# Weight layouts from the host, a first product paced by its loads, and program order on TensorE, ScalarE and VectorE in a one-core hybrid decoder layer

## The chip, the core and the metric

The kernel runs on one core of a Trainium2 chip. Its time is the device time of one execution on that core, in microseconds (us); what the host does with arrays before the launch is not in it. The core's engines run beside each other, each through its own list of instructions in order: TensorE (PE) for matmuls, VectorE (DVE), ScalarE (ACT) and GpSimd (POOL) for elementwise work, SyncE (SP) for issuing most of the DMAs. An instruction waits on semaphores for what it reads and for the buffers it writes.

## What is computed

One decoder layer on x of 256 positions by 2048 channels, all in float32:

```
x = x + 1/2 * SwiGLU_1(RMSNorm(x))             # FFN1, inner width 5632
h = RMSNorm(x); p = h @ W_in                   # columns: q|k, v, o, i, f gates, S5 input u
y = [ mLSTM heads | S5 groups ] @ W_out        # mixer
x = x + y
x = x + 1/2 * SwiGLU_2(RMSNorm(x))             # FFN2
out = RMSNorm_final(x)
swiglu(x) = (silu(x @ w1) * (x @ w3)) @ w2
```

The mLSTM part has four heads in chunks of 64 positions, after a causal convolution of width 4 and a silu on q and k. The S5 part is 64 groups of 16 channels, each driving a diagonal complex state of 64, with a scan over the positions, then a gelu and a gate through `w_glu`.

## The kernel before

**Products.** A float32 product is made from three passes of PE. Each weight tile, two blocks of 128 rows by 512 columns (512 KB, `wraw`), is split into a high part `whi` by an ACT cast (line 157) and a low part `wlo` by a DVE subtraction (line 159); the activations are kept as `xh` and `xl` in the same way. `step_tok` then issues twelve matmuls of 128x512 (line 177): four with whi and xh, four with whi and xl, four with wlo and xh. One such step, over two blocks of rows, is the unit in which the kernel counts. `gemm_ch` does the same for products with channels on partitions (lines 225, 226, 231), 24 matmuls of 128x256 a step.

**Loads ahead.** `weights` (line 143) keeps three further steps in flight (`AHEAD`): the DMA, cast and split of step i+3 are written into the program ahead of the matmuls of step i, with four buffers each of wraw, whi and wlo. The list of steps for that is `plan`. The last 512 columns of FFN2 are not in it; `tail` makes them in two halves of 256 columns, each of five tiles, by loads, casts (line 435), splits (line 436) and matmuls (lines 480 to 482) of its own, with an evacuation between the halves (line 445) and squares on ACT (line 323).

**Hooks.** After each step `tick` runs what `after(n, fn)` has put n steps ahead, and takes tasks from a background list at a rate: S5's tables during FFN1 (`s5_params`, `per_j`), S5's channel tasks in the mixer at `S5_RATE` tasks a step (`s5`: load, drive, scan, unrotate, emit, act, for eight groups j).

**Stages.** A setup; the first product of FFN1 (`start`), which takes x in its natural layout in four blocks, transposes them on PE (line 341, eight of 128x128 a block) between its steps, and takes squares of x on ACT; FFN1 until about 756 us; the mixer until about 1106 us, in the order U (S5's input, two halves, with the gate matmuls of line 928 between), O, QK, V, `w_out` for the heads' half, `w_glu`, `w_out` for S5's half; FFN2 until about 1801 us; the tail. In the mixer `gates` runs in three parts, `conv(hf, i)` for eight blocks, `scores(h)` for four heads (their masked products land in Dm, line 966), `heads(c)` and `heads_T(c)` for two pairs of heads (hml, line 1030, is the low part that `w_out` reads), `evac_glu` behind `w_glu`.

**Order.** SP's instructions stand in program order. On the other engines a scheduler orders the instructions by its own estimate of times, except in `start`, where PE, ACT and DVE are in program order too:

```
ET = mybir.EngineType
with tc.manual_schedule(engines={ET.SP}):
    _Layer(ctx, tc, a, out).run()
```

## Time and profile before

| what | us |
| --- | --- |
| median of 3 runs (1839.41 to 1839.99) | 1839.96 |
| the profiled execution, its own time | 1839.91 |
| its span | 1838.2 |
| PE busy | 1821.5 |
| DVE, ACT, POOL busy | 1064.4, 818.1, 348.9 |

The span is from the first to the last instruction; the 1.7 us beyond it lie around the profiled instructions. Busy time of PE counts pipelined matmuls by their modelled ends, so a PE that is busy without a break can still differ in the spacing of its matmuls; the granted clock (PEclk) says at how much of full speed it ran. A wait is put down to the semaphore that came last.

### The profile page before, as it was taken

What the parts mean: (1) busy time and instruction counts of PE and PEld (TensorE: products, weight loads), DVE (VectorE), ACT (ScalarE), POOL (GpSimd) and SP (SyncE); (2) the same over time, 40 slices, a digit from 0 to 9 for tenths busy, and PEclk for the clock granted to TensorE, in tenths of its full rate; (3) what the DMA queues carried; (4) which work ended last, traced back from release to release, by engine and by line L of the source; (5) the groups of instructions that cost most, each with busy time, mean ns of one, the idle gap of its engine ahead of it and who ended that gap; (6) DMA issues with size and microseconds to landing.
All of it is one profiled execution on the core that took longest, in us unless ns stands there. A gap on an engine that the chain in (4) does not pass through costs nothing.

```text
span 1838.2 us, 24018 instructions
## 1 busy us (share of the span) xinstructions
PE 1821.5 (99%) x9174; PEld 1527.0 (83%) x9174; DVE 1064.4 (58%) x1261; ACT 818.1 (45%) x982; POOL 348.9 (19%) x519
## 2 busy tenths in 40 slices
PE   9999999999999999999999999999999999999998
PEld 7888888888888888998977988888888888888887
DVE  5546855555555555578888665454544545454554
ACT  6444444334444445444454564444443334444343
POOL 4000799920000000065545100000000000000011
PEclk9999999999999999999999999999999999999999
DMA  8666676676666665767784556666665666666563
GB/s 275 196 186 185 192 217 214 213 242 196 196 197 195 188 198 195 198 181 208 184 211 149 190 189 201 193 192 189 189 187 192 193 194 191 189 193 186 193 193 128
DMA packets 185652, 358.26 MB, mean 195 GB/s; under 512 B 12064, under 2 KB 18336, under 8 KB 185408
## 3 DMA queue, kind: packets, MB, share of 16 engines
q1 hardware_dynamic: 181344, 344.51, 63.1%
q0 software_dynamic: 4048, 11.16, 1.7%
q8 instruction: 72, 1.18, 0.3%
q10 hardware_dynamic: 144, 1.05, 0.1%
q14 instruction: 44, 0.36, 0.1%
...
## 4 chain that ended last, share of the span: by engine, by line
PE 95%; DVE 2%; DMA 2%; issue 1%; ACT 0%; ACTq 0%; POOLq 0%; POOL 0%; SPq 0%; DVEq 0%
PE accb L177 84%; PE accb L225 2%; PE accb L231 2%; PE accb L226 2%; DVE wlo L159 1%; PE tpb L492 1%; DMA wraw<-in_w_in_dram 1%; PE tpb L341 0%; DMA wraw<-in_ffn_w_dram 0%; PE tpb L852 0%; PE accb L482 0%; PE accb L481 0%; PE accb L480 0%; PE tpb L891 0%; PE tpb L928 0%
## 5 line engine op out<-in xcount | busy, mean ns | idle before, releaser
L159 DVE TENSOR_TENSOR wlo<-wraw,whi 128x1024 fp32r<-128x1024 f32 x622 | 791.1, 1274 | 677.4 <-ACT whi L157 676.8
L157 ACT CAST whi<-wraw 128x1024 fp32r<-128x1024 f32 x622 | 654.4, 1053 | 885.3 <-PE accb L177 814.4
L177 PE MATMUL accb<-whi,xh 128*128 128x512 f32 x1536 | 603.5, 393 | 0.6 <-ACT whi L157 0.6
L177 PE MATMUL accb<-whi,xl 128*128 128x512 f32 x1536 | 598.9, 390 | 0.8 <-DVE xl L351 0.8
L177 PE MATMUL accb<-wlo,xh 128*128 128x512 f32 x1536 | 410.7, 389 | 0.0
L177 PEld LDWEIGHTS accb<-whi,xh 128*128 128x128 f32 x1536 | 289.0, 188 | 61.6 <-ACT whi L157 1.3
L177 PEld LDWEIGHTS accb<-whi,xl 128*128 128x128 f32 x1536 | 289.0, 188 | 60.3 <-DVE xl L351 1.6
L177 PEld LDWEIGHTS accb<-wlo,xh 128*128 128x128 f32 x1536 | 288.3, 188 | 60.1
L177 PE MATMUL accb<-whi,gh 128*128 128x512 f32 x664 | 259.8, 391 | 0.0
L177 PE MATMUL accb<-whi,gl 128*128 128x512 f32 x664 | 258.4, 389 | 0.0
L177 PE MATMUL accb<-wlo,gh 128*128 128x512 f32 x664 | 177.5, 389 | 0.0
L177 PEld LDWEIGHTS accb<-wlo,gh 128*128 128x128 f32 x664 | 124.6, 188 | 25.9
L177 PEld LDWEIGHTS accb<-whi,gh 128*128 128x128 f32 x664 | 124.6, 188 | 25.6
L177 PEld LDWEIGHTS accb<-whi,gl 128*128 128x128 f32 x664 | 124.7, 188 | 25.5
L1201 POOL TENSOR_TENSOR x<-x,fn 128x512 f32<-128x512 f32 x6 | 12.1, 2041 | 689.9 <-ACT junk L323 689.9
L703 POOL TENSOR_TENSOR tr<-s5rot,sp 128x128 f32<-128x128 f32 (+6 forms) x112 | 55.5, 496 | 160.2 <-DVE sp L643 156.7
L225 PE MATMUL accb<-xh,whi 128*128 128x256 f32 x256 | 63.5, 286 | 0.0
L226 PE MATMUL accb<-xl,whi 128*128 128x256 f32 x256 | 62.8, 283 | 0.0
L705 POOL TENSOR_TENSOR s5rot<-tr,tr 128x128 f32<-128x128 f32 (+6 forms) x112 | 61.0, 557 | 3.3
L704 POOL TENSOR_TENSOR tr<-s5rot,sp 128x128 f32<-128x128 f32 (+6 forms) x112 | 57.2, 511 | 0.0
L764 POOL DMA_DIRECT2D spillw<-s5w x16 | 8.6, 541 | 249.6 <-ACT s5w L735 239.2
L225 PEld LDWEIGHTS accb<-xh,whi 128*128 128x128 f32 x256 | 49.1, 192 | 0.8 <-issue 0.4
...
## 6 DMA issues: line engine op xcount, KB each, us to landing
wraw<-in_ffn_w_dram SPq DMA_DIRECT2D x528, 512.0 KB, 3.8
wraw<-in_w_in_dram SPq DMA_DIRECT2D x64, 512.0 KB, 5.7
wraw<-in_w_out_dram SPq DMA_DIRECT2D x32, 512.0 KB, 4.2
spillrot<-s5rot POOLq DMA_DIRECT2D x8, 512.0 KB, 5.4
...
s5rot<-spillrot SPq DMA_DIRECT2D x8, 512.0 KB, 6.9
...
wraw<-in_w_glu_dram SPq DMA_DIRECT2D x8, 512.0 KB, 3.7
```

The costliest lines, as they stand in the source:

```text
L157: nc.scalar.copy(hi, raw)
L159: nc.vector.tensor_sub(lo, raw, hi.bitcast(F32))
L177: nc.tensor.matmul(acc[t][:, :n], lhsT=x, rhs=wt, start=first and t not in seen, stop=last and t not in left)
L225: nc.tensor.matmul(o(nt), lhsT=wh[:, kk, ns(nt)], rhs=xh, start=st, stop=False, **kw)
L226: nc.tensor.matmul(o(nt), lhsT=wh[:, kk, ns(nt)], rhs=xl, start=False, stop=False, **kw)
L231: nc.tensor.matmul(o(nt), lhsT=wl[:, kk, ns(nt)], rhs=xh, start=False, stop=sp, **kw)
L492: nc.tensor.transpose(b[:, o:o + P], s[t][:, kt * P:(kt + 1) * P], self.ident)
L703: G.tensor_tensor(tr[0][:, :, :k], rv[:, 0, :, 0:k], u0, op=ALU.mult)
L704: G.tensor_tensor(tr[1][:, :, :k], rv[:, 1, :, 0:k], u1, op=ALU.mult)
L705: G.tensor_tensor(rv[:, a, :, k:2 * k], tr[0][:, :, :k], tr[1][:, :, :k], op=op)
L764: nc.gpsimd.dma_start(out=d, in_=t)
L1201: nc.gpsimd.tensor_tensor(self.x[c][:, t, :], self.x[c][:, t, :], self.fn[:, c * NC:(c + 1) * NC], op=ALU.mult)
```

## The change

**Layouts.** The host now hands over every weight as tiles of 512 KB in which each of the 128 partitions has 4 KB in a row, w_in's columns in the order in which the kernel uses them, x also as its transpose xT, all column vectors as one array of 128x112 (`cols`), the gate biases as one column, the gate weights with a partition's values in a row, S5's c tables already transposed and zero padded (1 MB where 0.5 MB were loaded), and the tail's weights as tiles (`w_last`). So the transposes of x in `start` (32, of which 24 stood behind the first product's first matmul), those of the vectors (lines 272, 294), and those of the c tables (line 734) are gone, and nine small DMAs of POOL became one.

**The first product.** `start` loads for each of its eight steps 256 KB of xT and the step's weights, splits both, and multiplies. xT has two buffers. The first weight tile comes in two halves. Warm-up matmuls are twelve at one place instead of eight and four. x in its natural layout is loaded during the next product, and squares, rstd and the first silu follow there.

**Order.** PE, ACT and DVE stand in program order throughout; POOL stays with the scheduler.

**Mixer tasks.** S5's low part (the subtraction to yl) is a task of its own, one round later, and the rate is 0.72 in place of 0.69. The gates come in five parts, a convolution block in three, scores of heads 0 and 1 within V's first half, heads(0), scores of 2 and 3, heads_T(0) in its second half, a scaling of the heads one step behind `heads`, `evac_glu` by pairs behind following steps.

The core of the diff:

```diff
-S5_RATE = 0.69
+S5_RATE = 0.72
...
-WARM = 8
-MORE_WARM = 4
+WARM = 12
...
+    def fetch(self, *step):
+        return self.split(self.load(*step))
+
+    def load(self, name, k, kk, c0, n, parts=1):
+        raw = self.wraw.tile([P, KK * NC], F32, name="wraw")[:, :kk * n].rearrange("p (k n) -> p k n", n=n)
+        m = kk // parts
+        for i in range(0, kk, m):
+            self.nc.sync.dma_start(out=raw[:, i:i + m, :], in_=self.wview(name, k, c0)[:, i:i + m, :])
+        return raw
+
+    def split_tiles(self):
+        return (self.whi.tile([P, KK * NC], F32R, name="whi"), self.wlo.tile([P, KK * NC], F32R, name="wlo"))
+
+    def split(self, raw, tiles=None, ks=None):
+        nc = self.nc
+        kk, n = raw.shape[1:]
+        hi, lo = (t[:, :kk * n].rearrange("p (k n) -> p k n", n=n) for t in tiles or self.split_tiles())
+        ks = ks or slice(0, kk)
+        nc.scalar.copy(hi[:, ks, :], raw[:, ks, :])
+        nc.vector.tensor_sub(lo[:, ks, :], raw[:, ks, :], hi[:, ks, :].bitcast(F32))
+        return hi, lo
...
+    def start(self, acc, fp):
+
+        nc = self.nc
         ET = mybir.EngineType
+        self.xh = [self.xTp.tile([P, 4, S], F32R, name=f"xh{c}") for c in range(4)]
+        self.xl = [self.xTp.tile([P, 4, S], F32R, name=f"xl{c}") for c in range(4)]
+        w, raw, ready = {}, {}, []
+
+        def load_xT(i):
+            raw[i] = fp.tile([P, NC], F32, name="s0").rearrange("p (k s) -> p k s", k=KK)
+            nc.sync.dma_start(out=raw[i], in_=self.a["xT"][:, KK * i:KK * (i + 1), :])
+
+        def load(i, parts=1):
+            w[i] = self.steps.pop(0)
+            w[i] = w[i], self.load(*w[i], parts=parts)
+
+        def split_x(k):
+            c, i = divmod(k, 4)
+            g, src = self.col("ffn1_norm", k), raw[k // KK][:, k % KK, :]
+            nc.scalar.activation(self.xh[c][:, i, :], src, AF.Copy, scale=g)
...
+        def prepare(i):
+            step, wr = w[i]
+            if i == 0:
+                tiles = self.split_tiles()
+                for kk in range(KK):
+                    split_x(kk)
+                    ready.append((step, self.split(wr, tiles, slice(kk, kk + 1))))
+                ready.pop()
+                return
+            if i < 8:
+                for kk in range(KK):
+                    split_x(i * KK + kk)
+            ready.append((step, self.split(wr)))
...
+            for i in range(2):
+                load_xT(i)
+                load(i, KK if i == 0 else 1)
+            prepare(0)
+            load_xT(2)
+            load(2)
+            prepare(1)
             for i in range(8):
-                M(i, W(i))
-                if i % 2 == 0 and i < 6:
-                    T(i // 2 + 1)
-                if i % 2 == 0 and i < 4:
-                    self.load_x(i // 2 + 2)
-                if i >= 4:
-                    self.sumsq(i - 4)
-        self.finish_rstd()
+                if i < 5:
+                    load_xT(i + 3)
+                if i + 3 < 10:
+                    load(i + 3)
+                if i < 7:
+                    prepare(i + 2)
+                else:
+                    prepare(9)
+                    self.load_x(0)
+                self.step_tok(acc, self.xs, [(i * KK, 0), (i * KK + 1, 0)], ready.pop(0)[1], NC, i == 0, i == 7)
+        self.ahead = ready
...
-    def wview(self, name):
-        return self.a[name][0].rearrange("(k p) n -> p k n", p=P)
+    def wview(self, name, k, c0):
+        c = WIN.index(c0) if name == "w_in" else c0 // NC
+        return self.a[name][c, k // KK]
...
-        vec0 = self.s5p.tile([KD, P], F32, name="vec0", tag="s5k0")
-        nc.sync.dma_start(out=vec0, in_=self.a["ffn1_norm"][0].rearrange("(k p) -> k p", p=P))
+        rows = sum(n for _, n in _COLS)
+        self.cols = c.tile([P, rows], F32, name="cols")
+        nc.sync.dma_start(out=self.cols, in_=self.a["cols"])
...
+                    s = []
+
+                    def silu(p1=p1, s=s):
+                        for t in range(TT):
+                            s.append(fp.tile([P, NC], F32, name=f"s{t}"))
+                            nc.scalar.activation(s[t], p1[t], AF.Silu, scale=self.rstd[:, t:t + 1])
                     if l == 1 and cc == 0:
-                        self.start(p1, w1, lambda k: self.cols0[:, k:k + 1])
+                        self.start(p1, fp)
+                        for i, n in ((1, 1), (2, 3), (3, 4)):
+                            self.after(n, lambda i=i: self.load_x(i))
+                        for i, n in enumerate((2, 3, 5, 6)):
+                            self.after(n, lambda i=i: self.sumsq(i))
+                        self.after(6, self.finish_rstd)
+                        self.after(6, silu)
                     else:
                         self.gemm_tok(p1, self.xs, w1, ks, cc * NC, NC)
-                    s = []
-                    for t in range(TT):
-                        s.append(fp.tile([P, NC], F32, name=f"s{t}"))
-                        nc.scalar.activation(s[t], p1[t], AF.Silu, scale=self.rstd[:, t:t + 1])
+                        silu()
...
-        craw = [sp.tile([P, NJ, 64], F32, name=f"craw{i}") for i in range(2)]
+        cT = sp.tile([P, 2, NJ, P], F32, name="cT")
...
-        load(out=self.wgr, in_=self.wview("w_in")[:, :, GATE0:GATE0 + 2 * H])
+        load(out=self.wgr, in_=self.a["wgr"])
...
-            load(out=craw[i], in_=self.a[nm][0].rearrange("(j r) h p -> (r h) j p", r=8))
+            load(out=cT[:, i], in_=self.a["cT"][i])
...
-                b2 = self.bank()
-                for ri in range(2):
-                    nc.tensor.transpose(b2[:, ri * P:(ri + 1) * P], stc[ri].rearrange("p g q -> p (g q)"), self.ident)
-                nc.scalar.copy(w2[:, 0:128], b2[:, 0:128])
-                nc.scalar.activation(w2[:, 128:256], b2[:, 128:256], AF.Copy, scale=-1.0)
+                nc.scalar.copy(w2[:, 0:128], cT[:, 0, j, :])
+                nc.scalar.activation(w2[:, 128:256], cT[:, 1, j, :], AF.Copy, scale=-1.0)
...
                 def act():
                     A.activation(yT[:, j, :], yT[:, j, :], AF.Gelu_apprx_tanh)
                     A.copy(yh[:, j, :], yT[:, j, :])
+
+                def low():
                     V.tensor_sub(yl[:, j, :], yT[:, j, :], yh[:, j, :].bitcast(F32))
-                return [load, drive, scan, unrotate, emit, act]
+                return [load, drive, scan, unrotate, emit, act, low]
...
-            for j in range(NJ + 1):
+            def both(f, g):
+                return lambda: (f(), g())
+            for j in range(NJ + 2):
                 now = s5_parts[j] if j < NJ else []
-                old = s5_parts[j - 1] if j else []
-                self.bg.extend(now[:3] + old[4:5] + now[3:4] + old[5:])
+                old = s5_parts[j - 1] if 0 < j <= NJ else []
+                low = s5_parts[j - 2][6] if j > 1 else None
+                if now:
+                    self.bg.append(both(low, now[0]) if low else now[0])
+                elif low:
+                    self.bg.append(low)
+                self.bg.extend(now[1:3] + old[4:5] + now[3:4] + old[5:6])
...
-            for i, part in zip((1, 8, 12), self.gates(ma, mp, gbank, rB, Dm, em)):
+            for i, part in zip((1, 2, 8, 11, 13), self.gates(ma, mp, gbank, rB, Dm, em)):
...
                 for i in range(4):
-                    self.after(1 + 2 * i, lambda hf=hf, i=i: conv(hf, i))
+                    for part in range(3):
+                        self.after(1 + 2 * i + part, lambda hf=hf, i=i, part=part: conv(hf, i, part))
...
+                self.after(1, lambda: scale_heads(c, den, ss))
+
+            def scale_heads(c, den, ss):
...
+                if c == 0:
+                    self.after(6, lambda: scores(0))
+                    self.after(7, lambda: scores(1))
...
                 if c == 0:
-                    for h, n in enumerate((1, 2, 5, 6)):
-                        self.after(n, lambda h=h: scores(h))
-                    self.after(4, lambda: heads(0))
-                    self.after(7, lambda: heads_T(0))
+                    self.after(3, lambda: heads(0))
+                    self.after(4, lambda: scores(2))
+                    self.after(5, lambda: scores(3))
+                    self.after(6, lambda: heads_T(0))
                 else:
                     self.after(1, lambda: heads(1))
                     self.after(4, lambda: heads_T(1))
...
+                if hf == 0:
+                    self.after(1, lambda: two(0))
+                    self.after(2, lambda: two(2))
+                else:
+                    two(0)
+                    self.after(1, lambda: two(2))
...
+        def scan_part():
             V.scalar_tensor_tensor(f, f, 0.0, e, op0=ALU.min, op1=ALU.subtract)
...
-            for h2 in range(2):
+        def matrix_part(h2):
+            if True:
...
-        return [rows_part, columns_part, matrix_part]
+        return [rows_part, scan_part, columns_part, lambda: matrix_part(0), lambda: matrix_part(1)]
...
-    with tc.manual_schedule(engines={ET.SP}):
+    with tc.manual_schedule(engines={ET.SP, ET.PE, ET.Activation, ET.DVE}):
...
+    a = {name: inputs[name] for name in _INS}
+    f = lambda name: _np.asarray(inputs[name][0])
+    cols = lambda v: v.reshape(-1, P).T
+    a["xT"] = f("x").T.reshape(KD, P, S).transpose(1, 0, 2)
...
+    win = [f("w_in")[:, c:c + NC] for c in WIN]
+    a["wgr"] = f("w_in")[:, GATE0:GATE0 + 2 * H].reshape(KD, P, 2 * H).transpose(1, 0, 2)
+    a["w_in"] = _np.concatenate(win, axis=1)[None]
+    W, k0 = NC // 2, HALVES[0] * 4
+    last = f("ffn2_w2")[k0 * P:, D - NC:].reshape(-1, 4, P, 2, W).transpose(3, 0, 2, 1, 4)
+    a["w_last"] = last
+    for name in _STEPS:
+        w = _np.asarray(a[name][0])
+        a[name] = w.reshape(w.shape[0] // (KK * P), KK, P, w.shape[1] // NC, NC).transpose(3, 0, 2, 1, 4)
+    return a
```

How instructions stand now, at three places; names are the program's, with the shape written (and how many times it stands in a row).

ACT near the end, before. `x_94` is the third block of x, whose evacuation and squares belong to the last full product; line 435 is the tail's cast.

```order
L323 ACTIVATE junk,ss<-x_93 128x512 x2
L157 CAST whi<-wraw 128x1024 x6
L435 CAST whi<-wraw 128x1024 x4
L435 CAST xh_14887<-wraw 128x1024
L323 ACTIVATE junk,ss<-x_94 128x512 x2
L435 CAST xh_14893<-wraw 128x1024
L435 CAST whi<-wraw 128x1024
L435 CAST xh_14899<-wraw 128x1024
```

ACT at the same place, after (line 468 is the tail's cast, 347 the square):

```order
L347 ACTIVATE junk,ss<-x_93 128x512 x2
L168 CAST whi<-wraw 128x1024 x7
L347 ACTIVATE junk,ss<-x_94 128x512 x2
L468 CAST whi<-wraw 128x1024 x5
L347 ACTIVATE junk,ss<-x_95 128x256 x2
L468 CAST xh_14793<-wraw 128x1024
L468 CAST xh_14799<-wraw 128x1024
L468 CAST xh_14805<-wraw 128x1024
L468 CAST xh_14811<-wraw 128x1024
L468 CAST whi<-wraw 128x1024
```

Four of the first half's five casts, and the first of the second half's, stood ahead of the squares of x_94; now all five stand behind them, and those of the second half behind the squares of x_95.

DVE between FFN1 and the mixer, before. Line 922 is the low part of the gate weights, line 410 an evacuation of FFN1; the evacuation of uT, line 809, comes 16 rows further down:

```order
L159 TENSOR_TENSOR wlo<-wraw,whi 128x1024
L922 TENSOR_TENSOR wg<-wgr,wg 128x16x4 x2
L159 TENSOR_TENSOR wlo<-wraw,whi 128x1024 x2
L410 SCALAR_TENSOR_TENSOR x_95<-accb,x_95 128x512 x2
L159 TENSOR_TENSOR wlo<-wraw,whi 128x1024
```

DVE after, in U's first half (line 829 is the evacuation of uT, line 951 the low part of the gate weights):

```order
L819 COPY rB<-tpb 128x256
L820 TENSOR_SCALAR hrstd<-rstd 128x2
L169 TENSOR_TENSOR wlo<-wraw,whi 128x1024
L829 TENSOR_TENSOR uT_6322<-accb,rB 128x2x128x2 x2
L951 TENSOR_TENSOR wg<-wgr,wg 128x16x4 x2
L169 TENSOR_TENSOR wlo<-wraw,whi 128x1024
```

The low part of the gate weights moved from FFN1's last steps to just behind the evacuation of uT, which waits for PE's last matmul ahead of the gate matmuls.

SP at the start, before (line 257 loads a block of x, 155 a weight tile):

```order
L256 DMA vec_96<-in_ffn_norm_dram 16x128
L257 DMA x_92<-in_x_dram 128x2x512
L155 DMA wraw<-in_ffn_w_dram 128x2x512 x2
L257 DMA x_93<-in_x_dram 128x2x512
L155 DMA wraw<-in_ffn_w_dram 128x2x512 x2
L257 DMA x_94<-in_x_dram 128x2x512
L155 DMA wraw<-in_ffn_w_dram 128x2x512 x2
L257 DMA x_95<-in_x_dram 128x2x512
L155 DMA wraw<-in_ffn_w_dram 128x2x512 x258
```

SP at the start, after (line 209 loads xT for one step, 157 a weight tile or half of one):

```order
L303 DMA cols<-in_cols_dram 128x112
L209 DMA s_226<-in_xT_dram 128x512
L157 DMA wraw<-in_ffn_w_dram 128x512 x2
L209 DMA s_231<-in_xT_dram 128x512
L157 DMA wraw<-in_ffn_w_dram 128x1024
L209 DMA s_245<-in_xT_dram 128x512
L157 DMA wraw<-in_ffn_w_dram 128x1024
L209 DMA s_257<-in_xT_dram 128x512
L157 DMA wraw<-in_ffn_w_dram 128x1024
```

A block of x of 512 KB for every two steps became 256 KB of xT for each step.

## Rows read from the trace of the kernel before

**Rows 1.** The page, part 1: busy us (share), instructions of each engine.

```profile
PE 1821.5 (99%) x9174; PEld 1527.0 (83%) x9174; DVE 1064.4 (58%) x1261; ACT 818.1 (45%) x982; POOL 348.9 (19%) x519
```

**Rows 2.** The chain of FFN2 from 1106 us: start, duration (us), work.

```profile
1106.11 43.54 PE accb L177 x192
```

**Rows 3.** Windows of 12 us, mixer: engines' busy us, PE clock, DMA share, GB/s.

```profile
820.00:832.00 12.00, 12.00 (x74) 9.17 (x73) 10.84 (x12) 1.48 (x2) 10.75 (x10) 0.86 0.54 144
...
940.00:952.00 12.00, 10.35 (x48) 8.28 (x46) 10.58 (x7) 5.22 (x8) 10.99 (x6) 1.00 0.72 206
952.00:964.00 12.00, 10.83 (x51) 8.47 (x52) 7.54 (x22) 4.85 (x12) 1.04 (x1) 0.86 0.76 218
964.00:976.00 12.00, 10.07 (x78) 8.10 (x76) 11.29 (x12) 4.59 (x8) 6.72 (x4) 1.00 0.27 89
976.00:988.00 12.00, 11.71 (x44) 9.43 (x45) 9.27 (x22) 7.59 (x17) 7.88 (x6) 0.86 0.67 225
```

**Rows 4.** Waits of PE from 820 to 1106: us in total, times, longest.

```profile
PE tpb L991 <- DVE Dm L966: 2.6, 1, 2.6
PE accb L177 <- DVE hml L1030: 2.2, 1, 2.2
```

**Rows 5.** Groups by line, ACT and DVE, 820 to 1106: busy, mean ns | idle before.

```profile
L157 ACT CAST whi<-wraw 128x1024 fp32r<-128x1024 f32 x87 | 90.4, 1046 | 67.8 <-PE accb L177 34.9 <-DMA wraw<-in_w_in_dram 20.9 <-PE accb L226 10.9
...
L159 DVE TENSOR_TENSOR wlo<-wraw,whi 128x1024 fp32r<-128x1024 f32 x89 | 129.1, 1460 | 43.0 <-ACT whi L157 43.0
```

**Rows 6.** The page, parts 5 and 6: DVE's splits; w_in loads, us to landing.

```profile
L159 DVE TENSOR_TENSOR wlo<-wraw,whi 128x1024 fp32r<-128x1024 f32 x622 | 791.1, 1274 | 677.4 <-ACT whi L157 676.8
...
wraw<-in_w_in_dram SPq DMA_DIRECT2D x64, 512.0 KB, 5.7
```

**Rows 7.** The chain of the start, 0 to 37 us: start, duration, work.

```profile
1.25 4.67 DMA x<-in_x_dram
...
11.65 8.45 DMA wraw<-in_ffn_w_dram
...
25.75 0.87 PE tpb L341 x8
```

**Rows 8.** Timeline of PE, first product: start, duration (us), work.

```profile
8.49 0.50 PE L177 MATMUL accb<-whi,xh 128*128 128x512 f32 x1 [0.57 <-ACT whi L157]
...
33.73 1.07 PE L177 MATMUL accb<-wlo,xh 128*128 128x512 f32 x4
```

**Rows 9.** Windows of 4 us at the start, columns as in rows 3.

```profile
8.00:12.00 4.00, 3.50 (x18) 2.95 (x19) 3.56 (x6) 2.74 (x5) 3.61 (x5) 1.00 1.06 403
12.00:16.00 4.00, 3.96 (x20) 3.01 (x19) 3.50 (x5) 2.95 (x6) 0.04 (x1) 1.00 1.11 289
```

**Rows 10.** Groups by line, FFN1: line 734 on PE.

```profile
L734 PE MATMUL tpb<-ident,stc 128*128 128x128 f32 x16 | 3.1, 273 | 0.0
```

**Rows 11.** Timeline around the gate matmuls: the splits of wg, uT, PE.

```profile
747.33 0.35 DVE L922 TENSOR_TENSOR wg<-wgr,wg 128x64 fp32r<-128x64 f32 x2
...
778.27 2.02 DVE L809 TENSOR_TENSOR uT<-accb,rB 128x512 f32<-128x512 f32 x2 [1.40 <-PE accb L231]
...
778.53 0.39 PE L928 MATMUL tpb<-xh,wg 128*36 128x256 f32 x2
```

**Rows 12.** Timeline near the end: block 1's evacuation, and the tail's middle.

```profile
1774.01 1.29 DVE L410 SCALAR_TENSOR_TENSOR x<-accb,x 128x512 f32<-128x512 f32 x2 [1.09 <-PE accb L177]
...
1776.12 1.03 ACT L157 CAST whi<-wraw 128x1024 fp32r<-128x1024 f32 x1
...
1777.18 1.48 DVE L159 TENSOR_TENSOR wlo<-wraw,whi 128x1024 fp32r<-128x1024 f32 x1 [0.76 <-ACT whi L157]
...
1815.47 0.78 DVE L445 SCALAR_TENSOR_TENSOR x<-accb,x 128x256 f32<-128x256 f32 x2 [0.40 <-PE accb L482]
...
1815.62 0.28 PE L480 MATMUL accb<-xh,gh 128*128 128x256 f32 x1
...
1816.85 0.19 ACT L323 ACTIVATION_READ_ACCUMULATOR junk<-x 128x1 f32 x1
```

145 lines of the change are left out of this document (60 added, 85 removed).

## The prediction

> **What bounds the kernel now.** I read the page's busy times first: TensorE (PE) is busy for 99% of the span [rows 1], so the time is the number of matmuls times their spacing, plus the places where PE waits or runs at half clock. The chain of FFN2 gives the spacing: 192 matmuls in 43.54 us, 0.2268 us each, 2.72 us for a step of twelve [rows 2]. The change removes hardly any matmul, so it can only touch the rest, and I looked for that rest stage by stage. Three places hold nearly all of it. In the **mixer**, the 12-us slices show lost PE time (10.35, 10.83, 10.07 and 11.71 us busy of 12) and a granted clock under 1 in three of them [rows 3]; the waits of PE there are two, 2.6 us for DVE's Dm (line 966) and 2.2 us for DVE's hml (line 1030) [rows 4]. At the **start** the first product's matmuls begin at 8.49 us, and its last four start at 33.73 [rows 8]. In the **tail** PE runs through: the first matmul of its second half starts at 1815.62, when the evacuation of its first half has just begun [rows 12]. So there is little to win in all, and any new wait of PE is paid in full.
>
> **Start.** Gone are 24 transposes of x between the first product's matmuls, three groups of 0.87 us [rows 7], and the stalls between them; x arrives transposed by the host. What comes late then is data. From the first x, landed at 1.25 + 4.67 = 5.92 [rows 7], and 403 GB/s [rows 9], 0.52 MB take 1.3 us, so moving counts from about 4.6 us. The first matmul needs cols, xT(0) and half of w(0), 0.58 MB: 4.6 + 1.45 = 6.05, then a cast of half of 1.03 us [rows 12]: about 6.7, where it was 8.49 [rows 8]. Step 1 has its data after 1.63 MB, at 4.6 + 4.05 + 1.05 = 9.7; bound by PE after that the product ends at 9.7 + 7 x 2.72 = 28.7, and I allow 0.5 for DVE's share: 29.2, against 33.73 + 4 x 0.227 = 34.64 [rows 8], a gain of 5.4. But each step now wants 0.79 MB, and the small loads of POOL (b, c, gates, 1.67 MB, the c tables twice as large as before) no longer stand behind nine small vectors and fall into the same time. To the last weight that is 8.0 MB. At 403 GB/s it is 20 us, no bound. At 289 GB/s, the rate of the 4 us in which the small loads were in flight, and in which one weight took 8.45 us to land [rows 7, 9], it is 27.7 us: landed at 32.3, cast 1.05, one step 2.72, end at 36.1, a loss of 1.5. I take the rate between, 346 GB/s, since the rows of 32 bytes are gone and those of 64 bytes stay: 23.1 + 4.6 + 1.05 + 2.72 = 31.5, a **gain of 3**; ends -5.4 and +1.5.
>
> **FFN1.** The 16 transposes of c (line 734) go [rows 10]. Their 273 ns are from start to end of pipelined ones; line 341's groups give 0.87 / 8 = 0.11 us of PE's time for one of the same form [rows 7], so 1.7 at most, and half of that if pairs overlap more closely. The transpose of the vectors goes too, 0.2. **Gain 1.3.** The order of DVE and ACT is now that of the code, with splits three steps ahead (8.2 us), which covers an evacuation of 1.29 us for two [rows 12]; POOL's order stays with the scheduler.
>
> **Mixer.** What can be won is what is lost: idle 1.65 + 1.17 + 1.93 + 0.29 = 5.0 us, and a clock of 0.86 in three slices of 12, 0.14 x 12 = 1.7 each, 5.1 [rows 3]; 10.1 in all. The half clock follows twice on the two long waits. Their causes: a split of w_in that came late, since its loads land after a median of 5.7 us and ACT's casts waited 20.9 us for them [rows 5, 6], and DVE, on which a split takes 1.46 us here against 1.27 over the run [rows 5, 6]. The change takes up both: contiguous w_in, scores and heads_T(0) a step earlier, S5's low parts a round later, the gates' matrix part in two. The waits themselves are not excluded, though: in program order a wlo behind a DVE operation that waits for POOL is late with it, and S5's tasks come at a rate of 0.72 instead of 0.69. I take **8** won; ends 4 (one long wait and its clock stay, 10.1 - 2.6 - 1.7 = 5.8, and some 2 more in short ones) and 10.1. Against it stand two new waits. DVE splits the gate weights (line 951) only behind the evacuation of uT; before, line 922 did that at 747.33, 31 us ahead [rows 11]. The evacuation takes 2.02 us from 778.27 and PE's third gate matmul stood at 778.53 [rows 11]: 778.27 + 2.02 + 0.18 - 778.53 = **1.9 lost**, 3.6 if the clock drops. And heads_T(1) is now followed at once by matmuls that read hm1, without S5's drive between: I take the ACT and DVE time of one tile, about **0.4**, between nothing and the 2.2 that hml cost before [rows 4].
>
> **Tail.** Here the scheduler had put the casts and splits of the tail's weights ahead of the squares and evacuations of the block before; the change's program order puts them behind, and the tail has no prefetch of its own. At its first half ACT must do both squares of x_94, which wait for DVE's evacuation, then the cast; DVE then the split, and only with it does PE's second matmul start. The same sequence stands one block earlier, where the prefetch hid it: evacuation from 1774.01, cast from 1776.12, split from 1777.18 for 1.48, done at 1778.66 [rows 12], 4.65 after its begin. As the row of 1815.62 shows, PE's next matmuls otherwise start with the evacuation: **4.5 lost**. At the second half: evacuation from 1815.47, last square done at 1817.04, cast 1.03, split 1.2 to 1.48, so 1819.3 to 1819.6 against the second matmul at about 1815.7: **3.6 lost** [rows 12]. Both are longer than the mixer's waits of 2.6 and 2.2, which were followed by a slice at 0.86 [rows 3, 4], so I add 1.7 for each: **11.5**; ends 8.1 (no clock lost) and 13.5 (POOL's products slow the splits too). TensorE's clock is 2.4 or 1.2 GHz by what the engine did before. By the Trainium skill, "TensorE: Matmul & The Clock Gate", section "HAM oscillation — how this bites in real kernels", waits of PE between groups of matmuls put the clock back to half, and the next group pays; that speaks against the change, and the trace agrees as far as the two waits above go. By that rule the tail costs the 11.5, without it 8.1.
>
> **Sum.** Against the profiled execution, 1839.91 us (span 1838.2 and 1.7 around it, 0.05 under the median of 1839.96): -3 - 1.3 - 8 + 1.9 + 0.4 + 11.5 = +1.5, so **1841.4**. What a measurement of this kernel can tell from no change is about 0.2%, 3.7 us: 1836.3 to 1843.6 count as the same.
>
> **Rivals.** A, *faster*: the first product is bound by PE (-5.4), the mixer wins all (-10.1), and the tail's waits cost no clock (+8.1): 1839.9 - 5.4 - 1.3 - 10.1 + 2.3 + 8.1 = 1833.5. For it: the layout does away with the mixer's worst waits. Against: DVE is 10.58 us busy of 12 in 940 to 952 [rows 3], so a late task has little room. 20%.
> B, *slower*: DVE behind POOL. Program order no longer lets DVE do a split while an S5 operation waits for POOL, and the splits are already slowed to 1.46 us there; the mixer wins only 4 while the tail costs all: 1839.9 - 3 - 1.3 - 4 + 2.3 + 11.5 = 1845.4. It decides from the point at which a wlo is more than its three steps, 8.2 us, late. For it: the busy DVE; against: the tasks were divided and moved later. By the Trainium skill, "GPSIMD Engine Reference", section "Key points", POOL shares its ways into SBUF with VectorE, and DVE instructions with two SBUF inputs contend; a split is one, and the trace's 1.46 against 1.27 us agrees. 22%.
> C, *slower too*: the small loads bound the first product (+1.5 in place of -3), rest as forecast: 1845.9. 8%.
> D, the change doesn't do what it says: casts and splits of the tail stand in another order than the code's, so the tail costs nothing: 1841.4 - 11.5 = 1829.9. Against it stands the printed order. 3%.
>
> **How the numbers follow.** The forecast, 1841.4 with its own range of 1836.3 to 1843.6, has 47%. Faster by over 0.2% is A and D, 23%; slower B and C, 30%. For 8 in 10 I go from 1833, past A's time, to 1846.5, past B's and C's; left out are D, and ends that add up, such as a mixer that wins 4 with two clock drops more.
>
> **What would show it.** In the profile after: ACT's rows of the tail with the casts behind the squares, and PE idle for about 4.5 us near 1801 and 3.6 near 1816, with clock under 1 after each; PE's wait for wg of about 1.9 after U0's first half; first matmul of the first product near 6.7 us, its last near 31.5, and DMA as what ends the waits between; in the mixer no wait for Dm or hml over 1 us. Wrong it is if PE waits in the mixer for wlo again and again (B), if the tail's gaps are short (D), or if FFN1 and FFN2, which I hold for untouched, move by more than 1 to 2 us.

## The result and the profile after

| what | before | after |
| --- | --- | --- |
| median, us | 1839.68 (1839.04 to 1839.99) | 1862.82 (1862.09 to 1864.65) |
| the profiled execution | 1839.91 | 1862.36 |
| its span | 1838.2 | 1860.3 |

The ratio is 1.0128, with a 95% interval of 1.0115 to 1.0141: the kernel became **slower by 23 us**, outside the range of 1833 to 1846.5. With marks at the start times of PE's rows (the first transposes of FFN1's inner activations, the first matmul of `dg` by ones in U's first half, the last gate matmul, FFN2's first matmul) the span divides into these stages, good to 0.1 us:

| stage | before | after | difference | forecast |
| --- | --- | --- | --- | --- |
| start, to FFN1's first transposes | 62.0 | 61.9 | -0.1 | -3 |
| rest of FFN1 | 713.0 | 711.8 | -1.2 | -1.3 |
| U's first half and gate matmuls | 8.8 | 10.7 | +1.9 | +1.9 |
| mixer, to FFN2's first matmul | 315.8 | 323.4 | **+7.6** | -8 + 0.4 |
| FFN2 and tail | 738.6 | 752.5 | **+13.9** | +11.5 |
| sum | 1838.2 | 1860.3 | +22.1 | +1.5 |

PE's busy time shows little, as the page counts it, against [rows 1]:

```profile
PE 1824.3 (98%) x9124; PEld 1526.6 (82%) x9124; DVE 1067.1 (57%) x1242; ACT 813.4 (44%) x985; POOL 341.9 (18%) x513
```

The waits of PE over the whole span of the kernel after (what PE waited for; us in total, times, longest) show it; `issue` means that the profile shows nothing that PE waited for. Of the two rows of before in the mixer [rows 4] the one for Dm is gone and the one for hml has shrunk to 0.6; the list is now this:

```profile
PE accb L187 <- ACT whi L168: 8.0, 7, 2.6
PE accb L187 <- DVE wlo L169: 4.5, 3, 3.0
PE tpb L872 <- issue: 3.4, 1, 3.4
PE accb L513 <- ACT whi L468: 3.0, 1, 3.0
PE accb L513 <- ACT xh L468: 2.2, 1, 2.2
PE tpb L957 <- DVE wg L951: 1.7, 1, 1.7
PE accb L514 <- DVE wlo L469: 1.6, 1, 1.6
...
PE accb L514 <- DVE xl L469: 0.9, 1, 0.9
PE accb L187 <- DVE hml L1066: 0.6, 1, 0.6
PE tpb L996 <- ACT qkc L991: 0.2, 1, 0.2
```

Lines 513 and 514 are the tail (7.7 us), line 957 the gates. Of the first row 5.4 us lie in the first product, and 2.6 in the mixer, where the waits come to 11.3 us with all three splits, line 872, hml and line 996; before they were 5.0. That is 6.3 of the mixer's 7.6. The clock cost about the same there as before: 6.8 and 3.4 us at half clock, against three times 3.4. The 12-us windows, as in [rows 3]:

```profile
832.00:844.00 12.00, 9.29 (x27) 7.00 (x27) 8.84 (x14) 5.50 (x8) 8.53 (x10) 0.72 0.61 219
...
940.00:952.00 12.00, 10.62 (x47) 8.08 (x45) 11.86 (x11) 2.80 (x4) 9.31 (x6) 1.00 0.51 175
952.00:964.00 12.00, 6.80 (x30) 5.19 (x28) 9.38 (x12) 10.84 (x18) 2.06 (x2) 1.00 0.57 187
964.00:976.00 12.00, 10.78 (x66) 8.89 (x70) 10.36 (x24) 4.66 (x13) 5.85 (x4) 0.86 0.41 132
```

PE is now idle for 5 us of 952 to 964, with DVE busy for 11.86 of the 12 us before.

**The tail** in the timeline (start, duration, work, in brackets the idle time before it):

```profile
1809.46 1.29 DVE L443 SCALAR_TENSOR_TENSOR x<-accb,x 128x512 f32<-128x512 f32 x2 [9.25 <-PE accb L187]
...
1811.56 3.87 ACT L468 CAST whi<-wraw 128x1024 fp32r<-128x1024 f32 x4
1812.62 4.21 DVE L469 TENSOR_TENSOR wlo<-wraw,whi 128x1024 fp32r<-128x1024 f32 x3 [1.88 <-ACT whi L468]
...
1812.64 0.38 PE L513 MATMUL accb<-whi,gh 128*128 128x256 f32 x1 [3.00 <-ACT whi L468]
...
1814.61 0.58 PE L514 MATMUL accb<-wlo,gh 128*128 128x256 f32 x1 [1.58 <-DVE wlo L469]
```

The evacuation, the two squares, then the cast, then the split, and PE behind each: the sequence that the prediction drew from [rows 12]. The windows of the two stretches behind the waits (columns as before; PEclk is the third number from the end) show both at half clock in this execution:

```profile
1813.70:1820.50 6.80, 5.89 (x27) 5.89 (x28) 4.26 (x4) 2.31 (x3) 0.00 (x0) 0.50 0.69 207
1834.20:1841.00 6.80, 5.92 (x28) 5.85 (x28) 5.53 (x5) 3.52 (x4) 0.00 (x0) 0.50 0.25 80
```

**The gates.** The split of wg (line 951) stands behind both evacuations to uT, and PE's third gate matmul waits for it:

```profile
776.93 1.94 DVE L829 TENSOR_TENSOR uT<-accb,rB 128x512 f32<-128x512 f32 x2 [1.01 <-PE accb L276]
...
778.72 0.33 DVE L951 TENSOR_TENSOR wg<-wgr,wg 128x64 fp32r<-128x64 f32 x2
...
779.11 0.42 PE L957 MATMUL tpb<-xh,wg 128*36 128x256 f32 x2 [1.75 <-DVE wg L951]
```

**The start.** The chain of 0 to 34 us is one of loads (`s` is xT's tile, whose two buffers come free with DVE's xl, so that two of these loads begin right behind an xl):

```profile
7.24 4.45 DMA s<-in_xT_dram
...
13.17 3.84 DMA s<-in_xT_dram
...
18.86 9.02 DMA wraw<-in_ffn_w_dram
```

One weight tile of 512 KB takes 9.02 us, where one of before took 8.45 [rows 7]. The windows of 4 us, as in [rows 9], tell the rate (last number):

```profile
8.00:12.00 4.00, 3.12 (x13) 2.27 (x14) 2.60 (x4) 2.25 (x4) 1.11 (x2) 1.00 0.98 278
12.00:16.00 4.00, 3.70 (x16) 2.73 (x15) 2.78 (x6) 3.22 (x6) 1.70 (x3) 1.00 0.97 282
```

PE's first matmul came at 6.14, ahead of the 6.7 that was forecast, and the last four of the product where they had been:

```profile
6.14 0.50 PE L187 MATMUL accb<-whi,xh 128*128 128x512 f32 x1 [0.34 <-ACT whi L168]
...
33.74 1.07 PE L187 MATMUL accb<-wlo,xh 128*128 128x512 f32 x4
```

### The profile page after: what moved, and what is told of

Read it like the earlier page. It is cut to its first block, busy times and chain, and to the rows that moved or that the text cites. A ratio compares the mean times of both kernels' runs of the same rounds, so it can differ in the third digit from the quotient of the medians.

```text
span 1860.3 us, 23875 instructions
## 1 busy us (share of the span) xinstructions
PE 1824.3 (98%) x9124; PEld 1526.6 (82%) x9124; DVE 1067.1 (57%) x1242; ACT 813.4 (44%) x985; POOL 341.9 (18%) x513
## 4 chain that ended last, share of the span: by engine, by line
PE 92%; DVE 4%; issue 1%; DMA 1%; ACT 1%; POOL 0%; SPq 0%; ACTq 0%; POOLq 0%; DVEq 0%
PE accb L187 82%; PE accb L270 2%; PE accb L271 2%; PE accb L276 2%; DVE wlo L169 1%; PE tpb L525 1%; DMA wraw<-in_ffn_w_dram 1%; DVE qkc L988 1%; PE accb L514 1%; PE accb L515 0%; PE accb L513 0%; DMA s<-in_xT_dram 0%; PE tpb L872 0%; DVE A L878 0%; PE tpb L365 0%
## 5 line engine op out<-in xcount | busy, mean ns | idle before, releaser
L169 DVE TENSOR_TENSOR wlo<-wraw,whi 128x1024 fp32r<-128x1024 f32 (+1 forms) x623 | 790.4, 1279 | 619.8 <-ACT whi L168 615.2
L168 ACT CAST whi<-wraw 128x1024 fp32r<-128x1024 f32 (+1 forms) x623 | 649.1, 1052 | 724.0 <-PE accb L187 645.4
L1254 POOL TENSOR_TENSOR x<-x,fn 128x512 f32<-128x512 f32 x6 | 7.6, 1290 | 694.6 <-ACT junk L347 694.6
L735 POOL TENSOR_TENSOR tr<-s5rot,sp 128x128 f32<-128x128 f32 (+6 forms) x112 | 47.4, 424 | 163.9 <-DVE sp L672 163.9
L734 POOL TENSOR_TENSOR tr<-s5rot,sp 128x128 f32<-128x128 f32 (+6 forms) x112 | 61.0, 545 | 3.7 <-DVE sp L675 0.2
L529 DVE TENSOR_TENSOR gl<-tpb,gh 128x512 fp32r<-128x512 f32 x44 | 28.3, 685 | 45.8 <-ACT gh L528 45.8
```

The costliest lines, as they stand in the source:

```text
L168: nc.scalar.copy(hi[:, ks, :], raw[:, ks, :])
L169: nc.vector.tensor_sub(lo[:, ks, :], raw[:, ks, :], hi[:, ks, :].bitcast(F32))
L529: nc.vector.tensor_sub(dl, b, dh.bitcast(F32))
L734: G.tensor_tensor(tr[0][:, :, :k], rv[:, 0, :, 0:k], u0, op=ALU.mult)
L735: G.tensor_tensor(tr[1][:, :, :k], rv[:, 1, :, 0:k], u1, op=ALU.mult)
```

## Experiments

"Mixer" is the time from the last gate matmul to FFN2's first, as above: 315.8 before, 323.4 after. Each run was compared with the kernel before on the same chip (1839.5 to 1840.2). The first question was whether the lost time stands where the order of the code puts it.

**The tail's splits ahead.** The kernel after, with the tail's first three tiles fetched behind the last steps of the block before, and the others as the tail goes:

```diff
+                    if l == 2 and hi_ == len(HALVES) - 1 and nc_ == 2:
+                        self.tails = []
+                        for i in range(3):
+                            self.after(7 + i, self.tail_fetch)
...
-                nc.scalar.copy(hi, raw)
-                V.tensor_sub(lo, raw, hi.bitcast(F32))
...
+                if len(self.tails) < 10:
+                    self.tail_fetch()
```

> The changed kernel, with the tail's tiles loaded, cast and split three steps ahead, as all other steps are; nothing else moves. Theory 'waits of the tail': the trace after shows PE idle 3.0 + 1.6 and 2.2 + 0.9 us at the tail's two halves and clock 0.5 for 6.8 us behind each, and the tail takes 42.3 us against 28.4 before. If casts behind squares are the cause, all 13.9 come back: about 1862.8 - 13.9 = 1849. Rival 'the tail's loads': its tiles land too late whatever the order of ACT, since the tiles are loaded only when buffers come free; then waits of ACT on the DMA take the place of the squares and less than 5 us come back, 1858 or more.

1850.15 us (1.0057, 1.0041 to 1.0074). FFN2 and tail take 738.7, so all but 0.2 of the 13.9 are back, and the slice that had 7.42 us of PE at a clock of 0.72 is full:

```profile
1809.00:1821.00 12.00, 12.00 (x94) 11.61 (x93) 7.79 (x8) 6.34 (x9) 2.55 (x2) 1.00 0.51 164
```

**The mixer by the scheduler, and the order alone.** The first is the kernel after with PE, ACT and DVE given back to the scheduler in the mixer; the second is the kernel before with all three in program order, and nothing else changed.

```diff
-        with self.tc.manual_schedule(engines={mybir.EngineType.PE, mybir.EngineType.Activation, mybir.EngineType.DVE}):
-            self.mixer(then(lambda k: self.col("ffn2_norm", k)))
...
+        self.mixer(then(lambda k: self.col("ffn2_norm", k)))
...
-    with tc.manual_schedule(engines={ET.SP, ET.PE, ET.Activation, ET.DVE}):
+    with tc.manual_schedule(engines={ET.SP}):
```

> The changed kernel, with the mixer alone given back to the scheduler on PE, ACT and DVE (FFN1 and FFN2 stay in program order; the divided tasks, the rate of 0.72 and the layouts stay). Theory 'order': from the gate matmuls on, the mixer loses 1.9 by the gate split and 7.6 more than before because in program order ACT's casts stand behind operations that wait for a late DVE; a scheduler that knows nothing of lateness still puts casts and splits ahead by its times, so the gate's wait goes and the mixer is at least as short as before: 1862.8 - 9.5 = 1853, and lower by what the contiguous w_in gives, down to 1846. Theory 'load on DVE': the divided tasks and the rate press more DVE work into O, QK and V than DVE can do, in any order; then only the gate's 1.9 come back, about 1861.

```diff
-    with tc.manual_schedule(engines={ET.SP}):
+    with tc.manual_schedule(engines={ET.SP, ET.PE, ET.Activation, ET.DVE}):
```

> The kernel before, with PE, ACT and DVE in program order throughout and nothing else changed: old layouts, old tasks, rate 0.69. Theory 'order': tail +13.9, gate +1.9, and the mixer at least 7.6 worse than before, since its parts are not divided: 1839.7 + 23.4 = 1863 or more, perhaps 1870. Theory 'load on DVE' (the new tasks and rate cost the mixer, not the order): only tail and gate, 1839.7 + 15.8 = 1855.5.

1854.1 (1.0076, 1.0061 to 1.0091), mixer 317.0, no wait for the gates; and 1869.97 (1.0164, 1.0149 to 1.0179), mixer 328.9, FFN2 and tail 752.6. So the order alone makes the tail's loss, and it costs the mixer 6.4 us with the tasks divided, and 13.1 with the old ones. But 317.0 is no gain over 315.8 either: under the scheduler something else in the change had eaten the better layouts.

**The small loads after the first product.** S5's, the convolution's and the gates' loads are issued by SP, behind the loads of the first product, in place of POOL:

```diff
-            tasks.append(lambda: nc.gpsimd.dma_start(**kw))
+            tasks.append(lambda: nc.sync.dma_start(**kw))
```

> The changed kernel, with the small loads (gate weights, S5's parameters, 1.67 MB) issued by SP in the order of the program, one every two or three steps after the first product, in place of POOL at once. Theory 'small loads bound the first product': steps 6 and 7 waited 1.6 and 1.7 us for casts whose weights took 9 us to land, and the start gained nothing (transposes of FFN1's first product end at the same 61.9 us); without the small loads the product is bound by PE: its waits go, 4.5 to 5.4 us come back, about 1858. Rival 'pacing': xT has two buffers and its load waits for DVE's use of the one before, so the loads come late anyway: under 1.5 us come back, 1861.5.

1857.9 (1.0099, 1.0084 to 1.0114); the start takes 57.8, so 4.1 us less. It holds in the other runs too: the seven profiles of kernels with the new start and early small loads have 61.7 to 65.1 us there, the eleven with late ones 57.1 to 58.9. PE's waits in the first 60 us, here and (second) in the kernel after:

```profile
PE accb L187 <- ACT whi L168: 0.7, 2, 0.5
```

```profile
PE accb L187 <- ACT whi L168: 5.4, 6, 1.7
```

**Layouts, division and rate apart.** All but the first product by the scheduler, small loads late; then the same with the tasks of the kernel before; and the two crossed with the other rate.

```diff
-    with tc.manual_schedule(engines={ET.SP, ET.PE, ET.Activation, ET.DVE}):
+    with tc.manual_schedule(engines={ET.SP}):
```

> The changed kernel (layouts, first product, divided mixer tasks, rate 0.72) with everything but the first product given back to the scheduler, as it was before, and the small loads by SP after the first product. Theory 'program order is what loses, the rest is as good as it was or better': from the kernel before, 1839.5, first product -4.2 and FFN1 -1.2 as in the run with late loads, gate and tail 0, mixer +1.2 as in the run whose mixer was scheduled: about 1835. Rival 'the layouts or the new start cost something that the order hid': 1839 or more.

```diff
-            for i, part in zip((1, 2, 8, 11, 13), self.gates(ma, mp, gbank, rB, Dm, em)):
+            for i, part in zip((1, 8, 12), self.gates(ma, mp, gbank, rB, Dm, em)):
...
-                    for part in range(3):
-                        self.after(1 + 2 * i + part, lambda hf=hf, i=i, part=part: conv(hf, i, part))
+                    self.after(1 + 2 * i, lambda hf=hf, i=i: conv(hf, i))
```

> As the run before it, and with the mixer's tasks as they were (not divided, rate 0.69): what is left of the change is the layouts and the first product. Theory 'w_in's slow loads made the mixer's waits' (the prediction's): contiguous w_in gives back most of the 10.1 lost there: 1839.5 - 5.4 - 8 = 1826. Rival 'VectorE's load made them': the mixer stays as before, 1839.5 - 5.4 = 1834, and the tasks' division is worth about 1 to the scheduler, one way or the other.

```diff
-S5_RATE = 0.72
+S5_RATE = 0.69
```

> As the scheduled kernel with divided tasks and late loads (1837.9), with S5's rate back at 0.69. With it the mixer, from the last gate matmul to FFN2, took 316.8 us; with the old tasks and rate 309.9. If the rate is what costs these 7 us: about 1831. If it is the division of the tasks (more places at which DVE's and ACT's work meets): it stays at 1838.

> The best so far (layouts, first product with late loads, scheduler, undivided tasks; 1832.0) with the rate at 0.72. If the rate costs the 7 us: 1839. If the division does: 1832, within 1.5.

> The scheduled kernel with divided tasks and late loads, rate 0.66. By the amount of DVE's work per step: no worse than 0.69 (1831.6), unless the last two or three tasks, which are then drained ahead of the gated product, cost by themselves up to 3 us: 1830 to 1834. By chance meetings: anything from 1830 to 1840.

> The same with rate 0.75. By the amount of DVE's work per step: worse than 0.72 (1837.9), some 1841 to 1846. By chance meetings: no such order, 1831 to 1840.

The table has the mixer's time, with the mean duration of the convolution's 24 multiply-adds on DVE ("taps", worked out from their rows):

| by the scheduler | rate | median (ratio, interval) | mixer | taps |
| --- | --- | --- | --- | --- |
| before (old layouts, undivided) | 0.69 | 1839.68 | 315.8 | 0.47 |
| undivided | 0.69 | 1832.04 (0.9958, 0.9943 to 0.9973) | 309.9 | 0.47 |
| undivided | 0.72 | 1841.95 (1.0013, 1.0003 to 1.0022) | 320.8 | 0.76 |
| divided | 0.66 | 1837.74 (0.9991, 0.9982 to 1.0001) | 317.8 | 0.67 |
| divided | 0.69 | **1831.56** (0.9958, 0.9943 to 0.9973) | 309.8 | 0.48 |
| divided | 0.72 | 1837.91 (0.9990, 0.9980 to 0.9999) | 316.8 | 0.76 |
| divided | 0.75 | 1847.66 (1.0047, 1.0032 to 1.0062) | 326.2 | 0.85 |

By the scheduler the layouts win 5.9 us of mixer; the division wins nothing at 0.69; the rate of 0.72 costs 7 to 11. With 0.69 and the scheduler the kernel is faster than both: **1831.56**. That 0.66 is worse than 0.69 speaks against mere amount of work per step; the rise from 0.69 over 0.72 to 0.75 doesn't, and 0.75 came out above what either theory had given it, so the rates alone don't decide between them.

The 5.9 are less than the 8 that were forecast, but the cause that was named for them is to be seen: ACT's casts waited 5.9 us for w_in's loads in the undivided kernel at 0.69, where they had waited 20.9 [rows 5], and no slice of its mixer is below full clock.

```profile
L168 ACT CAST whi<-wraw 128x1024 fp32r<-128x1024 f32 x90 | 93.5, 1047 | 66.5 <-PE accb L187 43.2 <-PE accb L271 12.8 <-DMA wraw<-in_w_in_dram 5.9
```

What else moved with the layouts (the mixer begins some 5 us earlier, the small loads come later) was not taken apart.

**The exponentials later.** In the kernel after, PE waits at 834.7 for a cast, because ACT stands at the exponential of Dm (line 1220) until DVE has done line 1219. After 14.10 us of idling ACT casts two tiles late:

```profile
832.25 0.52 ACT L1220 ACTIVATE Dm<-Dm 128x384 f32<-128x384 f32 x1 [14.10 <-DVE Dm L1219]
...
833.60 1.98 ACT L168 CAST whi<-wraw 128x1024 fp32r<-128x1024 f32 x2
...
834.69 0.80 PE L187 MATMUL accb<-whi,xh 128*128 128x512 f32 x1 [2.56 <-ACT whi L168]
```

```diff
+            def exp():
+                for hh in range(2):
+                    h = h2 * 2 + hh
                     A.activation(Dm[:, h, :], Dm[:, h, :], AF.Exp)
...
+            self.after(4, exp)
```

> The changed kernel, with the exponentials of Dm on ACT and POOL's masks four steps behind the DVE operations that feed them, in place of straight behind; nothing else. Theory 'ACT's casts stand behind exponentials that wait for a late DVE' (ACT waited 20.3 us for Dm, once 14.1): the wait of PE near 834, 2.6 us, and the half clock behind it, 3.4, go: 1862.8 - 6 = 1857. Rival 'DVE is late itself there': the splits come no earlier, and under 1.5 us come back: 1861.5.

1858.72 (1.0109, 1.0094 to 1.0124), mixer 320.0: 3.5 won. The wait for the cast went, and a shorter one for DVE's split came (1.9 us at the same place): 6.5 us in the mixer, where it was 4.5:

```profile
PE accb L187 <- DVE wlo L169: 6.5, 4, 3.0
```

So DVE itself is late there, with or without ACT behind it.

How a wait and the half clock hide one another shows at this place too. The kernel with the tail's splits ahead has the same mixer code. Its clock fell some 9 us later, for 3.4 us in place of 6.8, and PE, faster up to there, met a second late cast that the slow stretch had covered:

```profile
835.97 0.50 PE L187 MATMUL accb<-whi,xh 128*128 128x512 f32 x1 [2.56 <-ACT whi L168]
...
844.76 0.79 PE L187 MATMUL accb<-whi,xh 128*128 128x512 f32 x1 [2.60 <-ACT whi L168]
```

Its mixer took 323.8 all the same, against 323.4.

**Without the convolution's multiply-adds.** What makes DVE late from 940 to 960? The taps and the POOL instructions beside them, from the timelines of the two engines after:

```profile
939.52 2.55 DVE L988 SCALAR_TENSOR_TENSOR qkc<-qkp,cols,qkc 128x256 f32<-128x256 f32 x3
...
944.23 2.26 DVE L169 TENSOR_TENSOR wlo<-wraw,whi 128x1024 fp32r<-128x1024 f32 x1
...
948.64 4.37 DVE L988 SCALAR_TENSOR_TENSOR qkc<-qkp,cols,qkc 128x256 f32<-128x256 f32 x3
```

```profile
947.71 2.16 POOL L896 TENSOR_TENSOR S<-A,A 128x512 f32<-128x512 f32 x1
949.95 1.36 POOL L897 TENSOR_TENSOR A<-A,s5rot 128x512 f32<-128x512 f32 x1
951.27 1.46 POOL L898 TENSOR_TENSOR A<-A,s5rot 128x512 f32<-128x512 f32 x1
```

Three taps take 4.37 us beside POOL's S5 products. Of the 24 taps of this kernel the 17 that no POOL instruction overlaps took 472 to 486 ns, and the 7 that one overlaps 1384 to 1515; before, none was overlapped (from the rows of the two engines). Over all 24 (min/median/max ns, first and last start), after and then before:

```profile
L988 DVE SCALAR_TENSOR_TENSOR qkc<-qkp,cols,qkc x24: 472/485/1515, 899.5 to 957.8; 128x256 f32<-128x256 f32 x24
```

```profile
L957 DVE SCALAR_TENSOR_TENSOR qkc<-qkp,cols,qkc x24: 470/474/483, 895.0 to 930.9; 128x256 f32<-128x256 f32 x24
```

```diff
-                    for w in range(3):
+                    for w in range(0):
```

> The changed kernel without the 24 multiply-adds of the convolution on DVE (some 10 us of DVE's time in QK and V; the convolution is left out but for its last tap). Theory 'DVE's load': three of the chain's pieces between 932 and 952 are those operations, so the waits of PE near 946, 955 and 965 (1.2, 3.0 and 3.4 us) and the half clock behind them (1.7) go: 1862.8 - 9 = 1854. Rival 'the order, whatever the load' (splits behind operations that wait for POOL or ACT): the waits stay but for what the removed operations themselves took in front of them, under 3 us back: 1860.

1852.19 (1.0067, 1.0050 to 1.0084), mixer 313.7, that is 9.7 less; DVE's splits now keep PE for 0.4 us in the mixer where they kept it for 4.5:

```profile
PE accb L187 <- DVE wlo L169: 0.4, 1, 0.4
```

DVE's time in the convolution is what PE waits for from 940 to 970. The late casts ahead of the convolution (near 837 and 846 in this run) stay, with 3.9 us. The run doesn't tell whether 24 x 0.47 us would have fitted and only the stretching did not.

**Program order: the rate, the old tasks, and the mended kernel.** The kernel after with rate 0.69; with the undivided tasks of before (and 0.69); then with four mendings at once: the tail's splits ahead, the gates' split ahead of the evacuation, small loads late, exponentials later; and this at 0.69.

```diff
-            u_chunk(0)
             wg = mp.tile([P, 2, KD, GW], F32R, name="wg", tag="qkc")
...
+            u_chunk(0)
```

> The changed kernel with S5's rate at 0.69, nothing else. If the rate does in program order what it does under the scheduler (7 us), the mixer goes from 323.4 to 316.4 and the whole to 1856. If program order is the cause and the rate only adds to it there (a late DVE holds ACT in any case): 1861 to 1863.

> The changed kernel, all in program order, with the mixer's tasks undivided and the rate 0.69: the cell that is missing between the kernel before in program order (mixer 328.9, old layouts) and the changed one (323.4). If layouts give 5.9 here too and the division gives nothing to program order: mixer 323, the whole 1862. If it is the division that made program order bearable, and the layouts give nothing while DVE is late: mixer 329, the whole 1868.

> The changed kernel, in program order, with four mends at once: tail split three steps ahead (alone -12.7), gate weights split ahead of U (the 1.9 of its wait), small loads late (alone -4.9), exponentials of Dm four steps later (alone -4.1). If the causes are separate they add up: 1862.8 - 23.6 = 1839. If they hide one another (a DVE that is late all through the mixer eats what the mends give): 1843 or more.

> The program-order kernel with its four mends (1841.2) at a rate of 0.69. If the rate is the rest of the mixer's loss: 1841.2 - 7 to - 11 = 1830 to 1834, as good as the scheduled one (1831.6). If the order is: 1839 to 1841.

| in program order | rate | median (ratio, interval) | mixer | taps |
| --- | --- | --- | --- | --- |
| after | 0.72 | 1862.82 (1.0128, 1.0115 to 1.0141) | 323.4 | 0.76 |
| after | 0.69 | 1860.04 (1.0116, 1.0101 to 1.0131) | 323.0 | 0.80 |
| undivided | 0.69 | 1868.47 (1.0158, 1.0143 to 1.0174) | 329.3 | 0.84 |
| mended | 0.72 | 1841.24 (1.0009, 1.0000 to 1.0018) | 321.0 | 0.76 |
| mended | 0.69 | 1842.12 (1.0013, 1.0003 to 1.0022) | 322.5 | 0.80 |

The rate does nothing to the mixer here (the 2.8 us between the first two medians lie in the tail, where the clock of the second's profile fell once and not twice). The order costs 13.2 us of mixer at 0.69 (323.0 against 309.8), 19.4 with undivided tasks: what the division is good for is to make the order bearable. Nor do the layouts do anything here: undivided at 0.69 the mixer takes 329.3 with the new ones and 328.9 with the old. And the mended kernel shows that the single causes nearly add up: 13.9, 4.1, 3.5 and the gates' 1.9 make 23.4, and 21.6 were measured (13.2 in the tail, 4.0 at the start, 1.9 at the gates, 2.4 in the mixer).

**The phase.** By the scheduler short taps go with a short mixer in all rows so far. If that is a matter of which instructions meet, moving S5 by one task, at the same rate, should change it; if of the amount of S5 work, not. This is one line ahead of U's second half, under the scheduler and in the mended kernel:

```diff
             self.rate = S5_RATE
+            self.credit = -1
```

> The kernel whose mixer took 316.8 us under the scheduler at rate .72, with the same rate and S5's first task one task later. If what counts is which of the convolution's multiply-adds run beside POOL's S5 work (a matter of phase), their mean falls from .76 us towards the .48 us of the short mixers, the mixer takes about 310 us and the kernel about 1831. If it is how much S5 work a task carries, the shift does nothing: taps .76, mixer 316 to 317.5, kernel 1837 to 1839.

> The program-order kernel with its four waits mended (1841.2 us, mixer 321.0), with S5 one task later at the same rate. If phase decides in program order too: taps from .76 towards .48 us, mixer about 314, kernel about 1834. If the order itself holds VectorE late whatever the phase: mixer 320 to 322.5, kernel 1840 to 1843.

1833.0 (0.9960, 0.9945 to 0.9975) and 1835.79 (0.9976, 0.9966 to 0.9985). Under the scheduler the mixer falls from 316.8 to 311.9, and the taps, here, are as short as before:

```profile
L989 DVE SCALAR_TENSOR_TENSOR qkc<-qkp,cols,qkc x24: 470/472/485, 889.7 to 925.8; 128x256 f32<-128x256 f32 x24
```

The fastest kernel (scheduler, 0.69) shows how they can be: its taps run from 888.8 to 897 and from 916.9 to 925, and POOL's products stand between, from 899.6 to 915.8; they don't meet. So under the scheduler at 0.72 it is the phase that costs 4.9 of the 7.0. The shift moves all of S5's work, though, so the taps' share in it is not shown apart. In program order the shift won more (321.0 to 314.9), but not by the taps, which stay long:

```profile
L998 DVE SCALAR_TENSOR_TENSOR qkc<-qkp,cols,qkc x24: 471/485/1518, 888.4 to 947.0; 128x256 f32<-128x256 f32 x24
```

Of the 6.1 us some 4.6 can be seen: the waits of PE came to 9.1 us and are 6.2, and 10.2 us at half clock became 6.8. What went is the wait for a split at 829.9, with its half clock, and the one at line 881 (1.8 us); a shorter one (0.8) came:

```profile
829.92 1.20 PE L187 MATMUL accb<-wlo,xh 128*128 128x512 f32 x4 [1.94 <-DVE wlo L169]
```

The time came out as one theory had it, and by another way. Which instruction's move freed DVE at 830 was not settled.

## Why the prediction was wrong

**Right.** FFN1's transposes (-1.3 forecast, -1.2 measured); the gates (+1.9 forecast and measured, without a drop of the clock, and gone where the scheduler or a line moved puts the split ahead); heads_T(1) (0.4, and a wait of 0.6 for hml); FFN2 untouched. The tail's waits: 4.5 and 3.6 forecast, 4.6 and 3.1 measured, and for the cause that was named.

**The tail's clock was priced too low for this execution.** I added 1.7 for each of the two waits, the price of one slice at 0.86, which is 3.4 us at half clock. It was 6.8 us at half clock behind each, 3.4 lost. Waits of 7.7 and clock of 6.8 make 14.5; parts of the waits lie in the half-clock stretches and aren't lost twice, which goes with the 13.9 measured, just past the end of 13.5. But the next execution can do otherwise. In four of the runs above (the mixer by the scheduler, the small loads late, the exponentials later, and the kernel after at 0.69) the tail has the same code and, to 0.2 us, the same waits, and in their profiles the clock fell behind the first wait alone; FFN2 and tail took 10.7 to 11.6 us more than before, about the forecast's 11.5. With the small loads late that wait is there, but the 12 us behind it stand at full clock:

```profile
1829.77 0.38 PE L513 MATMUL accb<-xh,gh 128*128 128x256 f32 x1 [2.18 <-ACT xh L468]
```

```profile
1829.80:1841.80 12.00, 11.12 (x89) 10.77 (x90) 7.66 (x11) 5.44 (x8) 0.55 (x1) 1.00 0.15 45
```

The rows that I priced it from had waits of 2.2 to 2.6 us, but the length of the wait doesn't tell: in this mixer the 2.6 us at 834.7 went with 6.8 us at half clock, and the 3.4 us at 965.2 with 3.4. The ends should have gone from no such stretch to 6.8 us for each wait. The direction of the rule cited there, from the Trainium skill's "TensorE: Matmul & The Clock Gate", section "HAM oscillation — how this bites in real kernels", held behind the first wait of all eight profiles with this order in the tail, and behind the second in four of them.

**The start: the rate was taken too high.** I took 346 GB/s, the middle of 403 and 289; the slices have 278 and 282, and the product ended where it had (its last four matmuls start at 33.74, against 33.73): 0.1 won where I had 3. The loss of 1.5 that I had as the other end didn't come either, since later slices are faster (354 to 382 GB/s from 20 to 32). The small loads, C's mechanism, are the cause: moved away, they gave back 4.1, between my 3 and my best end of 5.4.

**The mixer is the step that failed.** "I take 8 won; ends 4 and 10.1" was a sum over losses that were there, with the plan that their causes go; 7.6 were lost. It was half right: without the order and at the old rate the new layouts do win 5.9, a 12-us slice below full clock is not to be found in that mixer, and even in the kernel after ACT waited only 8.8 us for w_in's loads in place of 20.9. But the ends bounded only what could be won. The two things that I named against it and left unpriced, a split behind a late DVE operation in program order and the rate of 0.72, were what turned the stage around. They are not a sum, since what each costs hangs on the other. Starting from the scheduler: the layouts -5.9, the division -0.1, the rate +7.0 (309.8 to 316.8), the order +6.6 (to 323.4). Starting from the order: the order +13.1 (315.8 to 328.9), the layouts +0.4, the division -6.3 (329.3 to 323.0), the rate +0.4. Either way it is +7.6. By the first way rate and order share the loss, by the second it is the order's: where it holds, neither the layouts' gain nor the rate's cost is to be seen. What makes a split late in that order is shown in part: the exponentials (3.5), the taps and what stretches them (the run without taps), and the phase (6.1). What released line 872 at 965.2, and which operations hold DVE back where the shift freed it, stays open.

Rival B had the mechanism, DVE beside POOL and PE waiting for wlo, and its sign, PE waiting in the mixer for wlo again and again, came true; but I let it lower the gain to 4, when it could as well turn the stage around: 10.1 us of losses bound what a stage can win, not what it can lose. The rule cited there, from the Trainium skill's "GPSIMD Engine Reference", section "Key points", did more than the 1.46 against 1.27 us of the splits: the taps, with two inputs in SBUF as well, went from 474 to as much as 1515 ns. I had that instruction at its undisturbed size before and didn't ask what would move beside it.

In all: of the 22.1 us, 13.9 are the tail, 7.6 the mixer, 1.9 the gates, and 1.3 were won at the start and in FFN1. Of the 20.6 us by which that misses the forecast of 1.5, the mixer makes 15.2, the start 2.9 and the tail 2.4.
